# Causal attentions of a three-layer decoder: spare projections tied to heads by issue order, their weights' low parts on GpSimd, and two more output tiles begun early

## The chip, the core and the metric

One NeuronCore of one Trainium2 chip runs the whole program in one launch. The metric is device time in microseconds (us) of that core. A profile comes from one execution of its own, whose time is given beside its span.

## What is computed

One sequence of 512 tokens, width 1024, goes through three layers, each with a mixer, a cross attention to 256 memory tokens and a feed-forward part. The mixers of the first and the third layer are causal attentions, and the change is in these two. Cut to that:

```python
def _hybrid_mixer(h, ...):                 # first layer
    qa, ka, va, qb, kb, vb, fl, ga, gb = split(h @ w_in)
    # 4 differential heads: two softmaxes each, (a1 - lam * a2) @ va
    # 8 forgetting-gate heads: softmax(qb kb^T / 8 + cum_q - cum_k, causal) @ vb
    merged = sigmoid(ga) * (ya @ w_diff_out) + sigmoid(gb) * (yb @ w_fox_out)
    return merged @ w_o

def mla_attention(h, ...):                 # third layer, 16 heads
    cq, ckv, k_pe = split(h @ w_dq_dkv)    # 384, 256 and 32 columns
    q = rmsnorm(cq) @ w_uq                 # per head 64 plain and 32 rotary columns
    k_nope, v = split(rmsnorm(ckv) @ w_ukv)
    s = (q_nope k_nope^T + q_pe k_pe^T) / sqrt(96)
    return concat(softmax(s, causal) @ v) @ w_o
```

Each cross attention needs keys and values `mem_n @ w_kv` of the memory, which depend on nothing else.

## The kernel before

**Numbers.** Every matrix is split into a high part (rounded by ScalarE) and a low part (the rest), and each product is three matmuls: high by high, low by high, high by low (`mm3`, L96 to L100). `weights` (L85) loads a tile of weights in pieces of up to 512 columns by SyncE's DMA queue into `raw` (6 buffers), casts the high part `wh` on ScalarE (L92) and subtracts the low part `wl` (L93) on VectorE, or on the engine that it is given. `wh` and `wl` have 3 buffers each. `proj` runs a projection: eight 128-row tiles by three, 24 matmuls of 512 columns.

**Banks.** PSUM has eight: `mm` 3 (projections), `s` 2 (scores), `tp` 2 (transposes), `pv` 1.

**A head.** For each of four query tiles: scores into an `s` bank (L340, or L603 and L604 in the first layer); `soft_rows` takes the masked maximum on VectorE (L278), scales it on GpSimd (L280, 128x1) and takes the exponential on ScalarE (L281); `soft` divides by the sum (L711, L712); `pt_fill` transposes on TensorE (L293) and copies high and low part out (L300, L301). Then `pv64` multiplies by V (L319 to L322) and adds the two halves into `y` (L325, L326), once per head. `pt_alloc` zeroes two blocks per head on GpSimd (L286). In the third layer `mla` subtracts the low part of a head's keys on GpSimd too (L1087).

**What sets the order.** The program is written as one list, and a planner at compile time lays it out for each engine: of the instructions that are ready in its own account of time, with a buffer for what they write, the one that stands first in the list is issued. On the chip each engine then takes its instructions in that fixed order. Work that waits for nothing is thus issued early, into any gap, however late it stands in the list.

**First layer (`mixer`).** Value projections, four differential heads, then eight forgetting-gate heads in four pairs; `qk_tiles` projects queries and keys of a pair (two projections), and the next pair's stand behind the pair in the list. After the heads come the gate projections: `gates(m)` makes two (columns of `ga` and `gb`), for m = 0 to 3 before anything that needs the heads' outputs. They depend on the normed input alone. `gated` multiplies a gate's sigmoid by the output projection `w_ab` of the first or the second kind of heads.

**Third layer (`mla`).** Five latent tiles are projected in order, m = 0 to 2 for queries and 3, 4 for keys and values, with the sum of squares of each kind in `acc`; `rstd` and `bcast` turn it into a norm by two small groups of matmuls (L115, L140). The key/value norm multiplies the keys of each pair (L1081) and V; the query norm goes into the tables that multiply the queries. Then come 16 heads in eight pairs: per two pairs one `proj_tok4` for V, per pair a key projection (6 matmuls), per head a query projection (9 matmuls, L348). Behind each pair stands one job for the last layer's cross attention, `mem_k` or `mem_v` in turn: 48 matmuls of 256 columns with two tiles of 1024 weight columns, and a store from GpSimd's queue. `mem_begin` prepares the memory behind the first pair.

**Output projection (`out_proj`).** Eight output tiles; the first `lead` of them are begun with the first `first` head pairs' outputs, before the last ones are there: three in `mm` banks, two in `s` banks. With `first=6` such a lead is 18 matmuls, its low parts are on GpSimd, and 6 more matmuls end it. In `mla` the leads stand behind all heads in the list. `split_y` (L78, L79) splits the heads' outputs.

Of the kernel before, what the change touches and what calls it, by code (L numbers as in the profile page):

```python
# [48 lines left out]
class Build:  # L49
# [46 lines left out]
    def mm3(self, out, l, r, start, stop):  # L96
        mm = self.nc.tensor.matmul
        mm(out, l[0], r[0], start=start, stop=False)  # L98
        mm(out, l[0], r[1], start=False, stop=False)  # L99
        mm(out, l[1], r[0], start=False, stop=stop)  # L100
# [235 lines left out]
    def scores(self, q, k, i):  # L336
        Sp = self.p("s")
        n = max(256, P * (i + 1))
        qs = slice(P * i, P * (i + 1))
        self.mm3(Sp[:, :n], (q[0][:, qs], q[1][:, qs]), (k[0][:, :n], k[1][:, :n]), True, True)  # L340
        return Sp
# [52 lines left out]
    def out_proj(self, chunks, ys, x, norm, gains, lead=0, first=4):  # L394

        h = first
        pss = []  # L400
        for m in range(lead):
            w = self.weights(chunks[m][:, :h * P], h * P, self.nc.gpsimd)
            ps = self.p("mm" if m < 3 else "s")
            self.proj(ps, w, ys[:h], stop=False)
            pss.append(ps)
        for m in range(KT):
            if m < lead:
                w = self.weights(chunks[m][:, h * P:], (len(ys) - h) * P)
                ps = pss[m]
                self.proj(ps, w, ys[h:], start=False)  # L410
            else:
                w = self.weights(chunks[m], len(ys) * P)
                ps = self.p("mm")
                self.proj(ps, w, ys)
            self.nc.vector.tensor_add(x[m], x[m], ps)
            self.norm_tile(norm, m, x[m], gains(m))
        self.norm_end(norm)
# [135 lines left out]
    def mixer(self, norm, x, nnorm, gains):  # L553
# [5 lines left out]
        def qk_tiles(name, h, bias=None):  # L559
# [4 lines left out]
            for i in range(2):  # L564
                ps = self.p("mm")
                self.proj(ps, self.weights(a[name][2 * h + i], 1024), xs)
# [31 lines left out]
        def scores(qk, hh, i):  # L598
            Sp = self.p("s")
            n = max(256, P * (i + 1))  # L600
            qs = slice(P * i, P * (i + 1))
            q, k, q2, k2 = (t[hh] for t in qk)
            nc.tensor.matmul(Sp[:, :n], q[:, qs], k[:, :n], start=True, stop=False)  # L603
            nc.tensor.matmul(Sp[:, :n], q2[:, qs], k2[:, :n], start=False, stop=True)  # L604
            return Sp
# [32 lines left out]

        Vb = self.proj_tok(a["w_vb"], 4, xs, r, "B", stacked=True)
        for pr in range(4):  # L640
            qk = nxt
            y = self.t("E")
            for hh in range(2):
                h = 2 * pr + hh
                PT = self.pt_alloc()
                for i in range(4):
                    self.soft(scores(qk, hh, i), i, self.mask, 0.125, PT)
                self.pv64(Vb[h // 4], PT, h, y)
# [12 lines left out]
        def gates(m, tag):  # L661
            gs = []
            for i in range(2):
                w = self.weights(a["w_gate"][2 * m + i], 1024)
                ps = self.p("mm")
                self.proj(ps, w, xs)
# [22 lines left out]
        early = [gates(m, "x") for m in range(4)]  # L689
# [332 lines left out]
    def mla(self, norm, x, nnorm, gains, mstats):  # L1022
# [3 lines left out]
        lat = []  # L1026
        acc = [self.t("acc"), self.t("P")]
        for m in range(5):
# [7 lines left out]
            lat.append((H, L))  # L1036
# [6 lines left out]
        cq, ckv = lat[:3], lat[3:]  # L1043
# [25 lines left out]
        ys = []  # L1069
        kv1 = None  # L1070
        for qt in range(4):
            V = self.proj_tok4(a["ukv_v"][qt], ckv, rkv, "xl")
            for pr in range(2):
# [9 lines left out]
                for hh in range(2):  # L1083
# [6 lines left out]
                    for i in range(4):  # L1090
                        self.soft(self.scores(q, kb, i), i, self.mask, scale, PT)
                    self.pv64(V, PT, 2 * pr + hh, y)
                ys.append(y)
                if kv1 is None:
                    kv1 = self.mem_begin("mem_2", "mem1", "kv1", ["xh"] * 8, mstats)
                (self.mem_k if pr == 0 else self.mem_v)(kv1, qt)
        self.out_proj([a["mla_o"][m] for m in range(KT)], self.split_y(ys), x, nnorm, gains, lead=5, first=6)
# [208 lines left out]
```

## Time and profile before

| | us |
|---|---|
| median of 3 runs (2336.34 to 2337.86) | 2336.62 |
| the profiled execution | 2336.24 |
| its span | 2334.3 |
| mean granted TensorE clock of the span | 0.992 |

The span runs from the first to the last instruction of the profiled execution; its own time is 1.9 us more. Engines are PE (TensorE matmul), PEld (its weight loads, which overlap), DVE (VectorE), ACT (ScalarE), POOL (GpSimd) and SP (SyncE, which issues most DMAs); a small q behind the name is the engine's sequencer. L12 is line 12 of the kernel. Tiles stand as out<-in by the program's names, so `pmm` is a bank of tag `mm`. A matmul's duration contains its way through the pipeline: two that follow each other overlap, and what one costs is read from the distance of their starts. The granted clock is 1.00 at 2.4 GHz and 0.5 at 1.2 GHz. Some matmul records are missing from a trace.

### The profile page before, as it was taken

To read this page: it belongs to the slowest core of one execution; us is meant where nothing else is said; L and a number is where in the kernel's file an instruction comes from. 1 tells how busy PE (TensorE), PEld (TensorE's weight loads), DVE (VectorE), ACT (ScalarE), POOL (GpSimd) and SP (SyncE) were. 2 spreads that over 40 slices of the span, in tenths; PEclk is the share of its full clock that TensorE was granted. 3 is DMA by queue.
4 is the path that set the end of the run, shared out by engine and by line. 5 is a ranking of instruction groups with operands and counts; after the bars stand their busy time and mean duration, and the time that the engine had idled before them with its cause. 6 is when DMAs were issued, how large, how long until landed. Compare 5 with 4: busy or idle time off the path is not lost.

```text
span 2334.3 us, 32205 instructions
## 1 busy us (share of the span) xinstructions
PE 2286.1 (98%) x11454; PEld 1935.8 (83%) x11454; DVE 1407.3 (60%) x2581; ACT 1038.8 (45%) x2064; POOL 561.9 (24%) x672
## 2 busy tenths in 40 slices
PE   8999989999999999989999999999999999999998
PEld 8888868888888888878888888887997888888887
DVE  6586774556645444966656654546997656555443
ACT  6476753455323225444543332235776454332222
POOL 5323211113201105983121110011234121110002
PEclk9999999999999999989999999999999999999999
DMA  8322123313332233343123333332321313333232
GB/s 302 108 72 74 63 91 108 105 53 124 100 99 94 96 100 109 99 145 119 62 97 100 96 94 99 97 98 91 122 90 62 102 50 111 100 99 97 93 93 70
DMA packets 130528, 232.50 MB, mean 100 GB/s; under 512 B 15078, under 2 KB 25446, under 8 KB 130240
## 3 DMA queue, kind: packets, MB, share of 16 engines
q1 hardware_dynamic: 127472, 221.41, 29.6%
q0 software_dynamic: 2752, 8.81, 1.0%
q8 instruction: 90, 1.47, 0.3%
q14 instruction: 70, 0.57, 0.1%
q10 hardware_dynamic: 144, 0.23, 0.0%
HBM read 221.93 MB, written 9.71 MB: 99 GB/s over the span
## 4 chain that ended last, share of the span: by engine, by line
PE 54%; DVE 1%; ACT 1%; issue 0%; DVEq 0%; POOL 0%; ACTq 0%
PE pmm L98 16%; PE pmm L99 16%; PE pmm L100 15%; PE ps L98 1%; PE ps L99 1%; PE ps L100 1%; PE ptp L293 1%; PE ppv L320 0%; PE ptp L140 0%; PE ppv L98 0%; PE ppv L100 0%; PE ppv L99 0%; PE ptp L534 0%; PE ppv L319 0%; PE ptp L115 0%; DVE E L1180 0%
## 5 line engine op out<-in xcount | busy, mean ns | idle before, releaser
L92 ACT CAST wh<-raw 128x512 fp32r<-128x512 f32 (+1 forms) x816 | 454.2, 601 | 780.7 <-PE pmm L99 564.2
L93 DVE TENSOR_TENSOR wl<-raw,wh 128x512 fp32r<-128x512 f32 (+1 forms) x719 | 514.3, 741 | 196.0 <-ACT wh L92 194.4
L100 PE MATMUL pmm<-xh,wl 128*128 128x512 f32 (+1 forms) x1624 | 626.2, 386 | 0.0
L98 PE MATMUL pmm<-xh,wh 128*128 128x512 f32 (+1 forms) x1624 | 626.1, 386 | 0.0
L99 PE MATMUL pmm<-xl,wh 128*128 128x512 f32 x1560 | 609.5, 391 | 0.0
L98 PEld LDWEIGHTS pmm<-xh,wh 128*128 128x128 f32 x1624 | 303.9, 187 | 61.3 <-DVE x L668 0.2
L100 PEld LDWEIGHTS pmm<-xh,wl 128*128 128x128 f32 x1624 | 303.9, 187 | 61.0
L99 PEld LDWEIGHTS pmm<-xl,wh 128*128 128x128 f32 x1560 | 291.7, 187 | 60.7
L99 PE MATMUL pmm<-B,wh 128*128 128x512 f32 (+1 forms) x698 | 263.1, 378 | 0.5 <-DVE B L79 0.5
L98 PE MATMUL pmm<-A,wh 128*128 128x512 f32 (+1 forms) x578 | 217.9, 384 | 2.9 <-ACT A L78 2.9
L100 PE MATMUL pmm<-A,wl 128*128 128x512 f32 (+1 forms) x578 | 220.2, 384 | 0.0
L982 POOL TENSOR_TENSOR tmp<-tmp,rbc 128x512 f32<-128x512 f32 x44 | 57.4, 1306 | 492.2 <-ACT tmp L981 492.2
L99 PEld LDWEIGHTS pmm<-B,wh 128*128 128x128 f32 x698 | 133.2, 191 | 24.1 <-DVE B L79 0.9
L158 POOL TENSOR_TENSOR acc<-acc,tmp 128x512 f32<-128x512 f32 x55 | 79.8, 1452 | 249.6 <-ACT tmp L157 248.9
L93 POOL TENSOR_TENSOR wl<-raw,wh 128x512 fp32r<-128x512 f32 (+1 forms) x97 | 120.7, 1269 | 74.4 <-ACT wh L92 50.8
L98 PEld LDWEIGHTS pmm<-A,wh 128*128 128x128 f32 x578 | 108.2, 188 | 23.6 <-ACT A L78 3.3
L100 PEld LDWEIGHTS pmm<-A,wl 128*128 128x128 f32 x578 | 108.4, 188 | 20.4
L1004 DVE TENSOR_TENSOR x<-x,pmm 128x512 f32<-128x512 f32 x45 | 30.9, 687 | 136.3 <-PE pmm L100 136.3
L99 PE MATMUL pmm<-D,wh 128*128 128x512 f32 x288 | 112.0, 389 | 0.0
L98 PE MATMUL pmm<-E,wh 128*128 128x512 f32 x280 | 108.9, 389 | 0.0
L100 PE MATMUL pmm<-E,wl 128*128 128x512 f32 x280 | 108.9, 389 | 0.0
L281 ACT ACTIVATE P<-P,sm 128x128 f32<-128x128 f32 (+3 forms) x128 | 72.2, 564 | 52.1 <-POOL sm L280 51.0
(427 smaller groups left out, 3878.1 us busy)
## 6 DMA issues: line engine op xcount, KB each, us to landing
raw<-in_up SPq DMA_DIRECT2D x176, 256.0 KB, 2.7
raw<-in_w SPq DMA_DIRECT2D x128, 256.0 KB, 2.7
raw<-in_down SPq DMA_DIRECT2D x80, 256.0 KB, 2.7
raw<-in_kv_k SPq DMA_DIRECT2D x48, 256.0 KB, 3.0
raw<-in_kv_v SPq DMA_DIRECT2D x48, 256.0 KB, 3.0
raw<-in_w_gate SPq DMA_DIRECT2D x32, 256.0 KB, 2.9
raw<-in_xq SPq DMA_DIRECT2D x32, 256.0 KB, 2.7
raw<-in_pc_in SPq DMA_DIRECT2D x24, 256.0 KB, 2.7
```

What stands on the lines that cost most here:

```text
L92: self.nc.scalar.copy(H[:, sl], raw)
L93: (eng or self.nc.vector).tensor_sub(L[:, sl], raw, H[:, sl].bitcast(F32))
L98: mm(out, l[0], r[0], start=start, stop=False)
L99: mm(out, l[0], r[1], start=False, stop=False)
L100: mm(out, l[1], r[0], start=False, stop=stop)
L158: (nc.vector if last else nc.gpsimd).tensor_add(acc, acc, q)
L281: nc.scalar.activation(P_[:, :n], P_[:, :n], AF.Exp, bias=nb, scale=scale, accum_out=sums[:, sc:sc + 1])
L293: nc.tensor.transpose(tp[:, j, :], P_[:, j * P:(j + 1) * P], self.ident)
L982: nc.gpsimd.tensor_mul(cc, cc, norm.rb)
L1004: nc.vector.tensor_add(x[m], x[m], ps)
```

## The change

- `mm3` returns its last matmul, and the score helpers keep it (`last_s`). `tc.issue_after(ins)` binds the instructions of its block that are on `ins`'s engine to be issued behind `ins`, in issue order only, without a wait for its result. All uses here bind TensorE's instructions.
- The two gate projections of m = 0 to 3 are bound to the eight forgetting-gate heads, one each, behind the last matmul of the head's first scores. Their weights' low parts, and those of the query and key projections of these heads (`bias` is given there), are subtracted on GpSimd.
- In `mla` the key/value latents are projected first, and the two `acc` buffers change places. The jobs 0 to 3 (`mem_k`) and 4 to 7 (`mem_v`) are bound behind the first scores of heads 1, 3, 5, 7, 9, 10, 12 and 13, with both tiles' low parts on GpSimd; `mem_begin` stands behind head 0.
- `out_proj` begins seven tiles in `mla`, the sixth and seventh in the `tp` banks. The first three are bound behind scores of tile 0 and 2 of head 14 and tile 1 of head 15. The number of matmuls stays as it was.

```diff
@@ -97,7 +97,7 @@
         mm = self.nc.tensor.matmul
         mm(out, l[0], r[0], start=start, stop=False)
         mm(out, l[0], r[1], start=False, stop=False)
-        mm(out, l[1], r[0], start=False, stop=stop)
+        return mm(out, l[1], r[0], start=False, stop=stop)
     def proj(self, ps, w, xs, off=0, m=P, start=True, stop=True):
@@ -337,7 +337,7 @@
         Sp = self.p("s")
         n = max(256, P * (i + 1))
         qs = slice(P * i, P * (i + 1))
-        self.mm3(Sp[:, :n], (q[0][:, qs], q[1][:, qs]), (k[0][:, :n], k[1][:, :n]), True, True)
+        self.last_s = self.mm3(Sp[:, :n], (q[0][:, qs], q[1][:, qs]), (k[0][:, :n], k[1][:, :n]), True, True)
         return Sp
     def head_tile(self, w, xs, rb, off=0):
@@ -391,7 +391,7 @@
                 outs.append(self.stack(ps[:, v, :], r[:, 2 * u + v:2 * u + v + 1], tag))
         return outs
-    def out_proj(self, chunks, ys, x, norm, gains, lead=0, first=4):
+    def out_proj(self, chunks, ys, x, norm, gains, lead=0, first=4, pins={}):
@@ -399,10 +399,13 @@
         h = first
         pss = []
         for m in range(lead):
-            w = self.weights(chunks[m][:, :h * P], h * P, self.nc.gpsimd)
-            ps = self.p("mm" if m < 3 else "s")
-            self.proj(ps, w, ys[:h], stop=False)
-            pss.append(ps)
+            with ExitStack() as c:
+                if m in pins:
+                    c.enter_context(self.tc.issue_after(pins[m].ins))
+                w = self.weights(chunks[m][:, :h * P], h * P, self.nc.gpsimd)
+                ps = self.p("mm" if m < 3 else "s" if m < 5 else "tp")
+                self.proj(ps, w, ys[:h], stop=False)
+                pss.append(ps)
         for m in range(KT):
             if m < lead:
                 w = self.weights(chunks[m][:, h * P:], (len(ys) - h) * P)
@@ -563,7 +566,7 @@
             res, second = [], [[None, None], [None, None]]
             for i in range(2):
                 ps = self.p("mm")
-                self.proj(ps, self.weights(a[name][2 * h + i], 1024), xs)
+                self.proj(ps, self.weights(a[name][2 * h + i], 1024, nc.gpsimd if bias else None), xs)
                 t = self.t("tmp")
                 nc.vector.tensor_mul(t, ps, rb)
                 X0, X1 = self.t("A", dt=F32R), self.t("A", dt=F32R)
@@ -601,7 +604,7 @@
             qs = slice(P * i, P * (i + 1))
             q, k, q2, k2 = (t[hh] for t in qk)
             nc.tensor.matmul(Sp[:, :n], q[:, qs], k[:, :n], start=True, stop=False)
-            nc.tensor.matmul(Sp[:, :n], q2[:, qs], k2[:, :n], start=False, stop=True)
+            self.last_s = nc.tensor.matmul(Sp[:, :n], q2[:, qs], k2[:, :n], start=False, stop=True)
             return Sp
         ys = []
@@ -636,6 +639,7 @@
             ys.append(y)
             nxt = qk_tiles("w_qka", h + 1) if h < 3 else qk_tiles("w_qkb", 0, bias)
+        begun = []
         Vb = self.proj_tok(a["w_vb"], 4, xs, r, "B", stacked=True)
         for pr in range(4):
             qk = nxt
@@ -645,6 +649,8 @@
                 PT = self.pt_alloc()
                 for i in range(4):
                     self.soft(scores(qk, hh, i), i, self.mask, 0.125, PT)
+                    if i == 0:
+                        begun.append(self.last_s)
                 self.pv64(Vb[h // 4], PT, h, y)
             ys.append(y)
             if pr < 3:
@@ -658,12 +664,15 @@
             slots += [d[:, S * j:S * (j + 1)] for j in range(3)]
         slots += [self.t("T", dt=F32R) for _ in range(6)]
-        def gates(m, tag):
+        def gates(m, tag, begun=None):
             gs = []
             for i in range(2):
-                w = self.weights(a["w_gate"][2 * m + i], 1024)
+                w = self.weights(a["w_gate"][2 * m + i], 1024, nc.gpsimd if m < 4 else None)
                 ps = self.p("mm")
-                self.proj(ps, w, xs)
+                with ExitStack() as c:
+                    if begun:
+                        c.enter_context(self.tc.issue_after(begun[2 * m + i].ins))
+                    self.proj(ps, w, xs)
                 t = self.t(tag)
                 nc.vector.tensor_mul(t, ps, rb)
                 gs.append(t)
@@ -686,7 +695,10 @@
             self.split(gs[0], H, L)
             merged.append((H, L))
-        early = [gates(m, "x") for m in range(4)]
+        early = []
+        for m in range(4):
+
+            early.append(gates(m, "x", begun))
         for i in range(2):
             for m in range(4):
                 gated(early[m], m, i)
@@ -1023,9 +1035,9 @@
         nc, a = self.nc, self.a
         xs, rb, r = norm.xs, norm.rb, norm.r
         scale = 1.0 / math.sqrt(96)
-        lat = []
-        acc = [self.t("acc"), self.t("P")]
-        for m in range(5):
+        lat = {}
+        acc = [self.t("P"), self.t("acc")]
+        for m in (3, 4, 0, 1, 2):
             w = self.weights(a["dq"][m], 1024)
             ps = self.p("mm")
             self.proj(ps, w, xs)
@@ -1033,14 +1045,14 @@
             tag = "B" if m < 3 else "A"
             H, L = self.t(tag, dt=F32R), self.t(tag, dt=F32R)
             self.split_scaled(ps, g, H, L)
-            lat.append((H, L))
+            lat[m] = (H, L)
             self.square_into(acc[m // 3], ps, m in (0, 3), m in (2, 4))
             if m == 2:
                 rqb = self.bcast(self.rstd(acc[0], 384, pre=r), tag="ty")
             elif m == 4:
                 rkv = self.rstd(acc[1], 256, pre=r)
                 rkvb = self.bcast(rkv, tag="G")
-        cq, ckv = lat[:3], lat[3:]
+        cq, ckv = [lat[m] for m in range(3)], [lat[m] for m in (3, 4)]
         w = self.weights(a["dpe"], 512)
         ps = self.p("mm")
         self.proj(ps[0:64, :], w, xs, m=64)
@@ -1066,8 +1078,17 @@
             nc.scalar.copy(t[no, :], rqb[no, :])
             nc.vector.tensor_mul(t[pe, :], rqb[pe, :], self.cs[pe, :])
             csr.append(t)
-        ys = []
+        ys, tiles = [], []
         kv1 = None
+        mem = lambda j: (self.mem_k if j < 4 else self.mem_v)(kv1, j % 4, (nc.gpsimd, nc.gpsimd))
+
+        def jobs(h):
+
+            j = {1: 0, 3: 1, 5: 2, 7: 3, 9: 4, 10: 5, 12: 6, 13: 7}.get(h)
+            if j is not None:
+                with self.tc.issue_after(tiles[4 * h].ins):
+                    mem(j)
+
         for qt in range(4):
             V = self.proj_tok4(a["ukv_v"][qt], ckv, rkv, "xl")
             for pr in range(2):
@@ -1089,12 +1110,15 @@
                     PT = self.pt_alloc()
                     for i in range(4):
                         self.soft(self.scores(q, kb, i), i, self.mask, scale, PT)
+                        tiles.append(self.last_s)
                     self.pv64(V, PT, 2 * pr + hh, y)
+                    if kv1 is None:
+                        kv1 = self.mem_begin("mem_2", "mem1", "kv1", ["xh"] * 8, mstats)
+                    jobs(2 * p_ + hh)
                 ys.append(y)
-                if kv1 is None:
-                    kv1 = self.mem_begin("mem_2", "mem1", "kv1", ["xh"] * 8, mstats)
-                (self.mem_k if pr == 0 else self.mem_v)(kv1, qt)
-        self.out_proj([a["mla_o"][m] for m in range(KT)], self.split_y(ys), x, nnorm, gains, lead=5, first=6)
+        lead = [(14, 0), (14, 2), (15, 1)]
+        self.out_proj([a["mla_o"][m] for m in range(KT)], self.split_y(ys), x, nnorm, gains, lead=7, first=6,
+                      pins={m: tiles[4 * h + i] for m, (h, i) in enumerate(lead)})
         return kv1
     def run(self):
```

## Rows read from the trace of the kernel before

**Rows 1.** Busy time of TensorE over the whole span (busy us, share, instructions).

```profile
PE 2286.1 (98%) x11454; PEld 1935.8 (83%) x11454; DVE 1407.3 (60%) x2581; ACT 1038.8 (45%) x2064; POOL 561.9 (24%) x672
```

**Rows 2.** Windows: length, busy us of five engines, granted clock, DMA share, GB/s.

```profile
223.80:291.60 67.80, 67.80 (x351) 57.10 (x350) 50.65 (x141) 46.20 (x103) 15.62 (x35) 1.00 0.22 69
291.60:312.70 21.10, 14.79 (x73) 10.24 (x72) 18.31 (x59) 14.26 (x39) 4.99 (x16) 0.92 0.04 13
...
1614.00:1626.10 12.10, 9.01 (x44) 7.63 (x45) 7.51 (x15) 8.46 (x16) 2.58 (x3) 0.86 0.16 51
1626.10:1635.30 9.20, 9.20 (x62) 8.38 (x61) 6.01 (x20) 5.87 (x13) 1.34 (x4) 1.00 0.38 129
...
1768.50:1796.10 27.60, 25.39 (x137) 20.45 (x137) 21.11 (x64) 19.99 (x52) 13.87 (x22) 1.00 0.09 31
1796.10:1826.00 29.90, 24.51 (x110) 19.11 (x109) 17.21 (x41) 13.70 (x33) 4.25 (x9) 0.89 0.21 67
1693.90:1742.40 48.50, 48.50 (x322) 44.21 (x321) 44.70 (x125) 34.34 (x88) 14.21 (x32) 1.00 0.28 88
```

**Rows 3.** Windows of TensorE's instructions on `pmm` alone: length, busy us (matmuls), clock.

```profile
223.80:291.60 67.80, 53.57 (x216) 1.00 0.22 69
291.60:312.70 21.10, 0.00 (x0) 0.92 0.04 13
...
1626.10:1635.30 9.20, 7.80 (x48) 1.00 0.38 129
```

**Rows 4.** Lines of VectorE: the add closing a head, 291.6 to 312.7; 1693.9 to 1742.4.

```profile
L326 DVE TENSOR_TENSOR E<-ppv,ty 64x512 f32<-64x512 f32 x3 | 2.1, 691 | 1.5 <-ACT ty L325 1.4
...
L326 DVE TENSOR_TENSOR E<-ppv,ty 64x512 f32<-64x512 f32 x4 | 2.7, 686 | 0.1
```

**Rows 5.** Waits of TensorE, 291 to 313 us (in total, times, longest).

```profile
PE ps L603 <- DVE sm L278: 3.7, 7, 0.9
PE ppv L322 <- DVE D L301: 1.3, 1, 1.3
```

**Rows 6.** Waits of TensorE, 1602 to 1626 us.

```profile
PE pmm L98 <- DVE tmp L1081: 2.4, 1, 2.4
PE ptp L140 <- DVE st L131: 0.8, 1, 0.8
```

**Rows 7.** Waits of TensorE, 1768 to 1826 us.

```profile
PE ptp L293 <- DVE D L301: 2.9, 2, 2.6
PE pmm L98 <- ACT A L78: 2.9, 2, 2.1
```

**Rows 8.** Timeline of TensorE: start, us, instruction; two projections, then MLA's first two heads.

```profile
849.78 0.39 PE L98 MATMUL pmm<-A,wh 128*128 128x512 f32 x1
...
850.46 0.39 PE L98 MATMUL pmm<-A,wh 128*128 128x512 f32 x1
...
1624.06 0.28 PE L98 MATMUL pmm<-xh,wh 128*128 128x256 f32 x1
1624.18 0.28 PE L99 MATMUL pmm<-xh,wh 128*128 128x256 f32 x1
...
1626.09 0.28 PE L98 MATMUL ps<-T,A 128*128 128x256 f32 x1
...
1635.29 0.28 PE L98 MATMUL ps<-T,A 128*128 128x256 f32 x1
```

**Rows 9.** Lines of VectorE, 1693.9 to 1742.4 us: low parts of weights (busy us, mean ns).

```profile
L93 DVE TENSOR_TENSOR wl<-raw,wh 128x512 fp32r<-128x512 f32 x14 | 10.3, 746 | 1.1 <-ACT wh L92 1.1
...
L93 DVE TENSOR_TENSOR wl<-raw,wh 128x256 fp32r<-128x256 f32 x2 | 0.8, 414 | 0.0
```

**Rows 10.** The page's groups: low parts of weights on GpSimd, whole span.

```profile
L93 POOL TENSOR_TENSOR wl<-raw,wh 128x512 fp32r<-128x512 f32 (+1 forms) x97 | 120.7, 1269 | 74.4 <-ACT wh L92 50.8
```

**Rows 11.** Timeline of GpSimd, 1794 to 1800 us.

```profile
1794.71 4.10 POOL L93 TENSOR_TENSOR wl<-raw,wh 128x512 fp32r<-128x512 f32 x4
```

**Rows 12.** Timeline of VectorE, 1796 to 1801 us.

```profile
1798.15 0.94 DVE L93 TENSOR_TENSOR wl<-raw,wh 128x256 fp32r<-128x256 f32 x1
```

## The prediction

> **What bounds the kernel now.** The first view is the busy table: TensorE is busy for 2286.1 us of a span of 2334.3 [rows 1], so only its idle time, and the time in which it runs at half clock, can be won. The windows say where that lies in the stretches that the diff touches [rows 2]. In the eight forgetting-gate heads, TensorE has no gap from 223.8 to 291.6 us, then 14.79 busy of 21.10: 6.31 idle, at a granted clock of 0.92. In the latent attention (MLA), 1614 to 1626.1 has 3.09 idle at 0.86, 1626.1 to 1635.3 none, 1768.5 to 1796.1 has 2.21 idle, and 1796.1 to 1826 has 5.39 idle at 0.89. A clock below 1.00 is a stretch of the 1.2 GHz level among 2.4 GHz; it loses (1 − granted) × stretch: 1.69 + 1.69 + 3.29 = 6.7 us. With the idle (17.0, and 0.8 just before 1614 [rows 6]) some 24 us are at stake.
>
> Next, what was done in the full stretch. 216 projection matmuls (pmm) ran from 223.8 to 291.6 us, and none from 291.6 to 312.7 [rows 3]. 216 is nine projections of 24: all eight early gates and one query/key projection. The spare work is spent by head 3, and heads 4 to 6 run bare: three closing adds in 21.1 us, so 7.0 us a head [rows 4], of which TensorE works 14.79 / 3 = 4.9. What it then waits for is the softmax: score banks that the VectorE maximum (L278) has to free, and the copies of the transposes [rows 5]. In MLA the memory's key and value jobs are the spare work, spent before the last four heads.
>
> **The change, part by part.**
>
> *Gates behind heads.* A 512-column matmul costs 0.68 / 3 = 0.227 us [rows 8], a gate of 24 of them 5.4. One per head makes 4.9 + 5.4 = 10.3 us of TensorE against a chain of 7.0: TensorE becomes the bound in all eight heads, and the clock has no cause to fall. Gates moved away from heads 0 to 3 only let those heads run sooner, since the total of matmuls is the same. At stake 6.31 + 1.69 = 8.0. I leave 1.3, one wait as long as the longest of this stretch [rows 5], for head 0, where only one gate covers the first softmax: **−6.7 us**.
>
> *Latents in the order 3, 4, 0, 1, 2.* Before, the key/value latent came last, and the query projections waited 2.4 us for L1081, which needs its norm, after 0.8 for that norm's own broadcast [rows 6]. Now that norm is ready three projections (16 us) earlier. The query norm is late instead, behind the rotary key, V and key projections, which hide it as they hid the other. −3.2 and −1.69 of clock: **−4.9 us**.
>
> *Memory jobs behind heads 1, 3, 5, 7, 9, 10, 12, 13.* The first job ran around head 0: 17 matmuls up to its first scores at 1626.09 and 31 more up to head 1's at 1635.29. At 0.12 us each [rows 8] its 48 matmuls are 5.7 us, and they filled head 0's softmax in a stretch without a gap [rows 2, 3]. Now head 0 has no cover but the next pair's key projection (6 × 0.227 = 1.4). The next pair's query weights must queue for one of three weight buffers behind the job's own two, so they are late too. Bounds: 0 if that projection still comes, and 5.7 + 1.7 for a clock drop if nothing does. Nearest is the job without the key projection: **+4.3 us**. The other jobs stand where a pair's projections leave room; heads 12 and 13, bare before (2.21 idle), get two: **−1.7 us**, with 0.5 left.
>
> *Three leads pinned into heads 14 and 15, two more in the transposes' banks.* A lead is 18 matmuls, 4.1 us. Three pinned ones give 12.3 us of cover where 2.6 us were spent on a transpose whose bank VectorE had not freed, and the two in the transposes' banks give 8.2 after the last transposes, over the 2.1 us wait for the last head's split [rows 7]. They start no earlier than that bank is free, which is before the last PV product, so they can cover it. At stake 5.39 + 3.29 = 8.7; with 1.3 left: **−7.4 us**. The two outputs' weights come in three pieces instead of two (one more ScalarE cast each), beside a full TensorE: 0.
>
> *Low parts on GpSimd.* 8 query/key, 8 gate and 8 × 2 job weights make 64 subtractions of 128x512, and two new leads 4 smaller ones. Each leaves VectorE (0.746 us [rows 9], 47.7 in all) and takes 1.27 on GpSimd [rows 10], 81 us over stretches where it is mostly idle. Behind them on its queue stand the 128x1 scaling of every softmax (L280), MLA's key low part, the zero blocks of the next head and the stores of the jobs; ScalarE's exponential waits for the scaling. Four such subtractions ran in a row for 4.10 us at 1794.71 [rows 11], just ahead of the 2.6 us wait. Bounds: 0 (where spare matmuls are at hand, as for 67.80 us in the gate stretch, a late softmax costs nothing; a gain is not excluded, as VectorE is relieved) and 2.6 per four for the 8 jobs, 20.8. Between them the nearest stretch is 1768.5 to 1796.1, where leads' low parts already share GpSimd with the heads: 2.21 idle over about ten of them, 0.22 each. Half of the jobs' and leads' 36 I take as covered: 18 × 0.22 = **+4.0 us**. The 32 others lie beside a full TensorE: 0.
>
> Sum: −6.7 − 4.9 + 4.3 − 1.7 − 7.4 + 4.0 = −12.4. The profiled execution took 2336.24 us (span 2334.3), 0.4 below the median of 2336.62; 2336.24 − 12.4 gives **2324 us**.
>
> **Where the skill speaks against it.** The row first: a 128x256 low part on VectorE took 0.94 us beside GpSimd's four [rows 12], against 0.41 at other times [rows 9]. The Trainium skill ("SBUF — State Buffer", Who interferes with whom) says that such a VectorE instruction and GpSimd share one port pair, an exclusive lock that blocks the loser for the whole instruction; by that rule the sum would be that of the third rival, and this row agrees with it.
>
> **The rivals.**
> 1. *The hole moves.* MLA heads without a spare job (0, 2, 4, 6, 8, 11) each idle as the bare gate heads did, 6.31 / 3 = 2.1 us: 12.6 in place of 4.3, giving 2332. For it: the same softmax, two score banks. Against: MLA heads are heavier on TensorE, 48.5 us for four with their jobs [rows 2, 4], and the pair's projections fall into the even heads. Chance 0.10.
> 2. *GpSimd becomes the wait*, slower. Each job's four subtractions hold up the scaling as at 1794.71 and cost 2.6, each gate's two half of it: 8 × 2.6 + 8 × 1.3 = 31.2 in place of 4.0, giving 2351. It outweighs the gains from (12.4 + 4.0) / 12 = 1.4 us per four. Against: that row had next to no spare matmuls beside it, the new stretches have. Chance 0.11.
> 3. *The lock.* Every one of 36 MLA subtractions delays a VectorE instruction by 0.94 − 0.41 = 0.53: 19 us, which takes back most of the 23.9 that VectorE gains there (32 × 0.746). Where a job or lead stands beside, TensorE hides it; six heads without one pay 19 / 16 each, some 7 us: 2331. Chance 0.05.
> 4. *The bindings bind nothing*, because the spare work ran that late anyway: 2336. The 216 and 0 of [rows 3] say otherwise: 0.02.
>
> **How the numbers follow.** The forecast has the rest, 0.72. A measurement of this kernel tells a change from none at about 0.2%, 4.7 us: faster is below 2331.9. The forecast's own range is 2312.4 (all 23.8 won) to 2331.9. Rivals 1, 3 and 4 end near or within 0.2%, rival 2 above. So faster 0.72, same 0.17, slower 0.11. The range 2313 to 2337 holds the forecast and rivals 1, 3 and 4, and leaves out rival 2 and the rim of the forecast.
>
> **What would show it.** Right: gate projections spread over all eight heads, one each, and idle below 2 us at clock 1.00 from head 0 to head 7; no wait for L1081 after the latents; idle between MLA's first scores and the second head's of 3 to 6 us; below 2 us from head 12 to the last split. Wrong: waits of TensorE on transposes or scores whose chain goes back to L280 behind L93 on GpSimd, a granted clock below 0.9 at MLA's first head, or gaps in the even heads that add up to the old ones.

## The result, and the profile after

The changed kernel takes 2374.91 us (median of 4 runs, 2373.77 to 2375.79) against 2337.24 of the kernel before on the same chip: a ratio of 1.0155, 95% interval 1.0143 to 1.0167. It is 37.7 us slower where the forecast was 12 faster. The profiled execution has a span of 2372.0 us; that of before had 2334.3.

The page of the changed kernel: the busy table, then two groups (columns as in [rows 1, 10]).

```profile
PE 2299.6 (97%) x11454; PEld 1941.5 (82%) x11454; DVE 1395.7 (59%) x2515; ACT 1042.2 (44%) x2066; POOL 646.0 (27%) x740
...
L93 POOL TENSOR_TENSOR wl<-raw,wh 128x512 fp32r<-128x512 f32 (+1 forms) x165 | 211.7, 1306 | 111.3 <-ACT wh L92 83.7
...
L281 ACT ACTIVATE P<-P,sm 128x128 f32<-128x128 f32 (+3 forms) x128 | 72.0, 563 | 82.4 <-POOL sm L280 81.4
```

GpSimd took over 68 low parts (165 instead of 97) and grew by 84 us, as reckoned (81). TensorE runs the same 11454 matmuls, yet is busy 13.5 us longer; by the two cuts below, some 8 us of that are half clock. In the last row, ScalarE's exponential waited 81.4 us for the scaling L280; before, the same row of the page ends in 51.0.

Where the time went, by windows of the changed kernel (columns as in [rows 2]):

```profile
226.70:297.80 71.10, 60.72 (x294) 48.51 (x293) 43.40 (x123) 45.09 (x100) 33.83 (x52) 0.95 0.20 60
...
1637.00:1645.00 8.00, 7.78 (x42) 6.38 (x42) 4.04 (x20) 3.81 (x13) 1.32 (x5) 0.70 0.01 2
1645.00:1800.00 155.00, 139.16 (x887) 123.14 (x885) 115.72 (x312) 99.72 (x243) 75.19 (x117) 0.97 0.28 85
...
227.00:350.00 123.00, 108.78 (x527) 86.87 (x526) 82.39 (x215) 75.48 (x166) 42.04 (x70) 0.97 0.19 58
1616.00:1882.00 266.00, 238.40 (x1383) 205.22 (x1382) 193.32 (x470) 165.84 (x388) 120.08 (x169) 0.96 0.28 85
```

The last two rows are cut by the work, from the first forgetting-gate scores to 10 us behind the last closing add, and from 20 us ahead of MLA's first scores to 20 behind its last closing add. The same cuts of the kernel before:

```profile
224.00:339.00 115.00, 108.11 (x538) 87.77 (x537) 88.04 (x230) 75.84 (x168) 24.94 (x54) 0.99 0.19 60
1606.00:1841.00 235.00, 224.19 (x1367) 197.20 (x1367) 194.24 (x502) 159.91 (x380) 74.18 (x132) 0.98 0.30 96
```

The gate heads became 8 us longer, with 14.2 us idle instead of 6.9, and MLA 31 us longer, with 27.6 idle instead of 10.8 and a granted clock of 0.96 instead of 0.98 (10.6 against 4.7 us lost). The other 8 of the 31 us are busy time of TensorE that no view here takes apart. The stretch that had no gap in the gate heads (67.8 us, [rows 2]) now has 10.4 us of idle in 71.1. Over most of MLA before had no gap of note:

```profile
1640.00:1768.50 128.50, 128.49 (x875) 118.51 (x874) 115.47 (x323) 92.99 (x234) 42.21 (x87) 1.00 0.32 103
```

From 1645 to 1800 the changed kernel has 15.8 us idle, some 11 of them in heads 2, 4, 6 and 8, which have no job of their own. Two of the signs that the prediction named for its failure are plain: a granted clock below 0.9 at MLA's first head (0.70 from 1637 to 1645), and gaps in the even heads. Of the third, waits whose chain goes back to L280 behind L93, the waits are there; what they go back to is traced below.

TensorE's waits in the changed kernel, 226 to 262, 1610 to 1645 and 1645 to 1800 us (in total, times, longest):

```profile
PE ps L606 <- DVE sm L278: 5.4, 2, 3.5
...
PE ps L98 <- ACT A L78: 5.6, 1, 5.6
...
PE ps L98 <- DVE sm L278: 9.3, 10, 2.1
...
PE ps L100 <- DVE A L79: 1.7, 2, 1.5
```

The first and third are scores that wait for a bank, on which a softmax's maximum (L278) is late; the second is MLA's first scores, which wait for the split of the query; the last is scores that wait for a query's low part (L79).

### The profile page after: what moved, and what is told of

Its sections match the earlier page's. It is cut to its first block, busy times and chain, and to the rows that moved or that the text cites. A ratio compares the mean times of both kernels' runs of the same rounds, so it can differ in the third digit from the quotient of the medians.

```text
span 2372.0 us, 32212 instructions
## 1 busy us (share of the span) xinstructions
PE 2299.6 (97%) x11454; PEld 1941.5 (82%) x11454; DVE 1395.7 (59%) x2515; ACT 1042.2 (44%) x2066; POOL 646.0 (27%) x740
## 4 chain that ended last, share of the span: by engine, by line
PE 52%; DVE 2%; ACT 1%; issue 1%; POOL 0%; DVEq 0%; POOLq 0%
PE pmm L98 15%; PE pmm L99 15%; PE pmm L100 15%; PE ps L98 1%; PE ps L100 1%; PE ps L99 1%; PE ptp L293 1%; PE ptp L140 0%; PE ppv L98 0%; PE ppv L99 0%; PE ppv L100 0%; ACT wh L92 0%; PE ptp L537 0%; PE ppv L320 0%; PE ptp L115 0%
## 5 line engine op out<-in xcount | busy, mean ns | idle before, releaser
L93 DVE TENSOR_TENSOR wl<-raw,wh 128x512 fp32r<-128x512 f32 (+2 forms) x653 | 468.0, 742 | 193.1 <-ACT wh L92 190.4
L99 PE MATMUL pmm<-B,wh 128*128 128x512 f32 (+1 forms) x682 | 256.2, 376 | 0.0
L93 POOL TENSOR_TENSOR wl<-raw,wh 128x512 fp32r<-128x512 f32 (+1 forms) x165 | 211.7, 1306 | 111.3 <-ACT wh L92 83.7
L100 PE MATMUL pmm<-A,wl 128*128 128x512 f32 (+1 forms) x562 | 214.2, 384 | 0.4 <-DVE wl L93 0.4
L98 PE MATMUL pmm<-A,wh 128*128 128x512 f32 (+1 forms) x562 | 212.3, 383 | 0.0
L100 PEld LDWEIGHTS pmm<-A,wl 128*128 128x128 f32 x562 | 105.4, 188 | 20.8 <-DVE wl L93 0.8
L281 ACT ACTIVATE P<-P,sm 128x128 f32<-128x128 f32 (+3 forms) x128 | 72.0, 563 | 82.4 <-POOL sm L280 81.4
```

The source lines that it names most:

```text
L93: (eng or self.nc.vector).tensor_sub(L[:, sl], raw, H[:, sl].bitcast(F32))
L100: return mm(out, l[1], r[0], start=False, stop=stop)
L281: nc.scalar.activation(P_[:, :n], P_[:, :n], AF.Exp, bias=nb, scale=scale, accum_out=sums[:, sc:sc + 1])
```

## The experiments

Each kernel is set against the kernel before on its own chip, whose median was 2337.2 to 2339.7; the difference of the two medians stands as +18.4 us or the like, and costs of parts are differences of these. First, two theories: GpSimd's queue does it, or the bindings.

### All low parts back on VectorE, bindings kept

```diff
-self.proj(ps, self.weights(a[name][2 * h + i], 1024, nc.gpsimd if bias else None), xs)
+self.proj(ps, self.weights(a[name][2 * h + i], 1024), xs)
-w = self.weights(a["w_gate"][2 * m + i], 1024, nc.gpsimd if m < 4 else None)
+w = self.weights(a["w_gate"][2 * m + i], 1024)
-mem = lambda j: (self.mem_k if j < 4 else self.mem_v)(kv1, j % 4, (nc.gpsimd, nc.gpsimd))
+mem = lambda j: (self.mem_k if j < 4 else self.mem_v)(kv1, j % 4)
```

> The changed kernel with all 64 low parts back on VectorE; every binding, the latents' order and the seven leads stay. If the binding costs the time (theory B: the spare work stands in one block behind a head's first scores and is missing in the heads without it), the 38 us stay almost whole: 2360 to 2380 us, with the holes of the even MLA heads (2.5 to 3 us of TensorE each) still there. If GpSimd's queue costs it (theory G: the scaling of the maximum waits behind the subtractions), most comes back: 2325 to 2342 us.

2356.53 us, +18.4; ratio 1.0082 [1.0066, 1.0099]. Half of the loss is left.

### No binding, low parts on GpSimd; and neither

The first takes away all three uses of `issue_after`; the second takes away the bindings and the low parts on GpSimd, so that the order of the latents, the places of the jobs in the list and the seven leads are left.

```diff
-early.append(gates(m, "x", begun))
+early.append(gates(m, "x"))
-with self.tc.issue_after(tiles[4 * h].ins):
-    mem(j)
+mem(j)
-lead=7, first=6, pins={m: tiles[4 * h + i] for m, (h, i) in enumerate(lead)})
+lead=7, first=6)
```

> The changed kernel without any binding; low parts stay on GpSimd, the order of the latents, the jobs' places in the list and seven leads stay. Theory B: 2325 to 2342 us, no hole over 1 us before MLA's last heads. Theory G: 2360 to 2380 us, with the scaling L280 still waiting up to 4 us behind L93 on GpSimd.

2337.66 us, −0.4; 1.0002 [0.9992, 1.0011].

> The changed kernel without bindings and with the 64 low parts on VectorE; the latents' order, seven leads and the jobs' places in the list stay. If GpSimd costs time only where bound work leaves a softmax bare, this equals the run without bindings within 5 us: 2331 to 2338 us. If GpSimd's subtractions cost the 18 us by themselves that they cost beside the bindings: some 2320 us.

2330.27 us, −7.4; 0.9967 [0.9953, 0.9980].

The four corners: +37.7 (both), +18.4 (bindings), −0.4 (GpSimd), −7.4 (neither). The bindings cost 26 us by themselves; GpSimd's low parts cost 7 without them and 19 beside them, so 12 us come only where both are there. Both theories hold, that of the bindings more. The cuts by the work, of the kernel with the bindings only, then with neither:

```profile
224.00:340.00 116.00, 107.42 (x537) 87.25 (x536) 87.84 (x230) 76.40 (x168) 23.87 (x54) 0.99 0.19 58
1606.00:1863.00 257.00, 236.66 (x1385) 202.95 (x1383) 198.86 (x503) 165.86 (x389) 79.82 (x137) 0.97 0.28 88
```

```profile
226.00:342.00 116.00, 109.60 (x536) 88.78 (x535) 87.71 (x230) 76.08 (x168) 24.33 (x54) 0.96 0.19 59
1612.00:1840.00 228.00, 222.57 (x1376) 196.44 (x1375) 193.15 (x498) 161.30 (x383) 80.89 (x137) 1.00 0.31 97
```

The bindings add 29 us to MLA and nothing to the gate heads. GpSimd's 19 beside them (spans of 2372.0 and 2353.1) are 3 ahead of the first gate scores, 7 in the gate heads and 9 in MLA; what lies between and behind the cuts is the same within 0.1 us. The exponential's row of the page, of the kernel with the bindings only, with GpSimd only, and with neither, does not add up in this way:

```profile
L281 ACT ACTIVATE P<-P,sm 128x128 f32<-128x128 f32 (+3 forms) x128 | 72.0, 563 | 78.9 <-POOL sm L280 77.9
```

```profile
L281 ACT ACTIVATE P<-P,sm 128x128 f32<-128x128 f32 (+3 forms) x128 | 72.1, 563 | 65.3 <-POOL sm L280 64.3
```

```profile
L281 ACT ACTIVATE P<-P,sm 128x128 f32<-128x128 f32 (+3 forms) x128 | 72.2, 564 | 54.4 <-POOL sm L280 53.8
```

GpSimd's low parts raise the wait for the scaling L280 by 10.5 us without the bindings, but only by 3.5 beside them, where they cost most. In the changed kernel's two cuts it is 18.0 and 44.3 us, against 19.3 and 43.4 with the bindings only. So the wait for the scaling does not by itself account for the 19 us.

GpSimd's fixed order does hold the scaling up, as its timeline at the first gate head shows (start us, us):

```profile
226.23 5.02 POOL L93 TENSOR_TENSOR wl<-raw,wh 128x512 fp32r<-128x512 f32 x4
231.22 0.22 POOL L280 TENSOR_SCALAR sm<-sm 128x1 f32<-128x1 f32 x1
```

The maximum that L280 scales was there at 227.28 us; a scaling of 0.22 us stood 3.9 us behind four low parts. Little of this reaches TensorE here. Lines of ScalarE, VectorE and TensorE up to TensorE's next hole:

```profile
229.89 1.14 ACT L92 CAST wh<-raw 128x512 fp32r<-128x512 f32 x2 [3.56 <-issue]
231.47 0.40 ACT L281 ACTIVATE P<-P,sm 128x128 f32<-128x128 f32 x1 [0.45 <-POOL sm L280]
...
237.29 0.69 DVE L677 TENSOR_TENSOR x<-pmm,rbc 128x512 f32<-128x512 f32 x1 [4.50 <-PE ptp L293]
...
239.18 1.64 DVE L577 TENSOR_TENSOR A<-tmp,A 64x512 fp32r<-64x512 f32 x1
...
241.13 0.54 DVE L278 CUSTOM_DVE_ANT_0 P<-ps,mask 128x384 f32<-128x384 f32 x1
...
241.73 0.38 PE L606 MATMUL ps<-A,A 128*128 128x256 f32 x1 [3.55 <-DVE sm L278]
```

The first line is two casts of weights, which stood ahead of the exponential on ScalarE until 231.03; so the exponential waited only 0.45 us for the scaling. The scores at 241.73 wait for the maximum at 241.13. In VectorE's order that stands behind a gate's multiplication (L677), which waited 4.50 us for TensorE, and behind L577, which took 1.64 us beside GpSimd's low parts where the kernel with the bindings only has 0.69. That second way, VectorE's longer instructions, is measured under "The lock" below.

### Latents alone, leads alone, both

Each is the kernel before with that part of the change, the leads without `pins`.

```diff
-for m in range(5):
+for m in (3, 4, 0, 1, 2):
...
```

> The kernel before with the latents in the order 3, 4, 0, 1, 2 alone. By the prediction's step the 3.2 us of idle and 1.7 us of clock before MLA's first query projections go: 2332 us. If the query norm, now last, takes the place of the key/value norm as the wait (in the changed kernel TensorE waited 5.6 us for a split A L78 there): 2337 to 2341 us.

2333.55 us, −4.6; 0.9980 [0.9971, 0.9990]. Of the waits of [rows 6] one is left, in this kernel from 1595 to 1632 us:

```profile
PE pmm L98 <- DVE tmp L1081: 1.3, 1, 1.3
```

Its window from 1614 to 1626.1 us has a granted clock of 1.00 instead of 0.86.

```diff
-ps = self.p("mm" if m < 3 else "s")
+ps = self.p("mm" if m < 3 else "s" if m < 5 else "tp")
...
-... lead=5, first=6)
+... lead=7, first=6)
```

> The kernel before with seven leads in MLA's output projection instead of five, nothing bound. By the prediction's step the last 2.1 us wait for the split of the last head goes: 2334 to 2335 us. If the two more leads only take weight buffers and GpSimd's time from the last heads: 2337 to 2341 us.

2335.63 us, −2.5; 0.9988 [0.9979, 0.9998]. Its window at the end of MLA:

```profile
1796.10:1826.00 29.90, 27.46 (x126) 21.81 (x125) 13.34 (x34) 13.50 (x33) 9.56 (x15) 0.89 0.20 62
```

Idle 2.4 instead of 5.4 [rows 2], at the same clock of 0.89.

> The kernel before with the latents' order and seven leads alone. If the two gains add (0.2% and 0.12% alone): 2330 to 2332 us. If both fill the same wait at the end of MLA: 2333 to 2336 us.

2329.44 us, −8.2; 0.9964 [0.9951, 0.9976]: the two add up. At the end of MLA its half clock is gone too:

```profile
1792.00:1822.00 30.00, 28.70 (x139) 23.05 (x138) 14.12 (x37) 14.13 (x35) 9.52 (x12) 1.00 0.23 70
```

### Jobs behind other heads

The jobs' and the query/key low parts are on VectorE (the gates' stay on GpSimd), the jobs stand behind the even heads, which had none.

```diff
-j = {1: 0, 3: 1, 5: 2, 7: 3, 9: 4, 10: 5, 12: 6, 13: 7}.get(h)
+j = {0: 0, 2: 1, 4: 2, 6: 3, 8: 4, 10: 5, 12: 6, 13: 7}.get(h)
...
```

> The changed kernel with the low parts of queries, keys and jobs on VectorE (those of the gates stay on GpSimd) and the first six memory jobs bound behind heads 0, 2, 4, 6, 8, 10 instead of 1, 3, 5, 7, 9, 10. Theory: the even head is bare, because the projections of its pair have to come before it and the job comes after it; with the job behind its own first scores MLA's holes of 20.6 us fall to 8 or less and the time to 2338 to 2346 us. Rival: a block of 48 matmuls leaves holes behind whichever head it is bound to: 2350 us or more.

2359.54 us, +21.9; 1.0093 [1.0079, 1.0107]: no better than behind the odd heads (+18.4); MLA's cut is 259 us against 257. The theory that the choice of head is at fault falls; a job bound as one block costs about the same behind either.

### Pieces instead of blocks

A block of 24 or 48 matmuls covers the softmax of one score tile; the other three of the head have none. Here, with all low parts on VectorE and the leads free, each gate is bound in four pieces of six matmuls, one behind each score tile of its head, and each job in eight pieces behind the eight tiles of its pair.

```diff
-if i == 0:
-    begun.append(self.last_s)
+begun.append(self.last_s)
...
-with ExitStack() as c:
-    if begun: c.enter_context(self.tc.issue_after(begun[2 * m + i].ins))
-    self.proj(ps, w, xs)
+for k in range(8):
+    with ExitStack() as c:
+        if begun: c.enter_context(self.tc.issue_after(begun[4 * (2 * m + i) + k // 2].ins))
+        sl = slice(k * P, (k + 1) * P)
+        self.mm3(ps, (w[0][:, sl], w[1][:, sl]), xs[k], k == 0, k == 7)
...
```

> Low parts on VectorE, leads not bound, but gates and jobs bound in pieces: a gate's 24 matmuls six behind each of the four score tiles of its head, a job's 48 six behind each of the eight score tiles of a pair, and the job placed in the list behind the pair. Theory (the block is what costs): the holes of the gate heads fall below 4 us and those of MLA below 8, 2322 to 2332 us. Rival (held-back work occupies the three weight buffers, and the next pair's query weights come late): MLA's holes stay at 15 us or more, 2345 to 2360 us.

2338.56 us, +0.9; 1.0003 [0.9994, 1.0012]. Its two cuts by the work:

```profile
226.00:336.00 110.00, 106.16 (x536) 87.18 (x536) 86.87 (x230) 75.55 (x168) 23.48 (x54) 0.98 0.20 62
1602.00:1846.00 244.00, 227.71 (x1376) 199.42 (x1375) 197.74 (x503) 163.80 (x388) 79.26 (x136) 0.99 0.29 92
```

The gate heads are 5 us shorter than before, with 3.8 idle in place of 6.9; MLA is still 9 us longer, with 16.3 idle in place of 10.8.

The gate pieces alone, jobs and leads free:

> No binding in MLA, low parts on VectorE, latents in the new order, seven leads, and the gates bound in pieces of six matmuls behind each score tile of their heads. By the run in pieces the first layer's heads end 4 to 5 us sooner than unbound: 2325 to 2328 us. If what they win is paid back behind them: 2329 to 2332 us.

**2325.04 us, −14.7; 0.9935 [0.9923, 0.9948]**, the fastest kernel of this study. Its cuts:

```profile
226.00:336.00 110.00, 106.14 (x537) 87.15 (x536) 86.84 (x230) 75.98 (x168) 23.06 (x54) 0.98 0.20 62
1606.00:1834.00 228.00, 222.59 (x1376) 196.45 (x1375) 193.19 (x498) 161.30 (x383) 80.89 (x137) 1.00 0.31 97
```

MLA with free jobs: 5.4 us idle, clock 1.00. The binding of the jobs, in pieces, costs the 16 us between the last two kernels, which is also the difference of their MLA cuts (244 and 228).

The leads' binding without the others (low parts on VectorE):

> The run without bindings and with low parts on VectorE, plus the changed kernel's binding of the first three leads behind heads 14 and 15. If the leads belong to the bound work that costs time: 2334 us or more. If the last two heads have room for them, as the prediction had it: 2326 to 2331 us.

2329.77 us, −9.9; 0.9959 [0.9945, 0.9973]. Against −7.4 without it that is no loss, and with intervals that overlap no sure gain. Its cuts, the base for what bound gates and jobs cost:

```profile
224.00:340.00 116.00, 109.91 (x536) 89.04 (x536) 87.83 (x230) 76.31 (x168) 24.19 (x54) 0.96 0.19 58
1610.00:1839.00 229.00, 222.83 (x1375) 197.31 (x1373) 194.07 (x497) 161.16 (x383) 81.54 (x137) 0.99 0.31 96
```

### Why bound jobs cost in MLA

First suspect: the weights of a bound job hold two of the three weight buffers while the next pair's query weights wait. Here a job's weights go through the two buffers of tag `T` that MLA's keys leave free (four of six hold keys), one piece of 512 columns at a time; first with the jobs in pieces, then as one block behind the heads of the change:

```diff
+def piece(self, src, i):
+    H, L = self.t("T", dt=F32R), self.t("T", dt=F32R)
+    raw = self.t("raw")
+    self.nc.sync.dma_start(raw, src[:, S * i:S * i + S])
+    self.split(raw, H, L)
+    return H, L
...
```

> The run in pieces (low parts on VectorE, gates and jobs in pieces, leads not bound), with the jobs' weights in two idle buffers of tag T, 512 columns at a time, so that held-back jobs no longer occupy the three weight buffers that the next pair's queries need. If those buffers are what still costs in MLA (16.3 us of holes, mostly TensorE waiting for the split of a late query projection): holes of 8 us or less, 2322 to 2330 us. If it is something else: 12 us or more, 2335 to 2340 us.

2348.05 us, +8.4; 1.0038 [1.0024, 1.0051].

> Jobs again in one block behind the first scores of heads 1, 3, 5, 7, 9, 10, 12, 13, but with weights of their own in the T buffers; gates in pieces, low parts on VectorE, leads not bound. If the late query weights alone made the holes, MLA's fall to 8 us or less, about 2325 to 2332 us. If the block makes most of them: 14 us or more, 2338 to 2352 us.

2374.33 us, +34.6; 1.0149 [1.0133, 1.0164]. Both are slower than with the shared buffers (+0.9 in pieces, +18.4 as blocks with the gates and leads bound too), so the theory gets no support. It is not excluded: with two buffers, which also take the jobs' split results, a job's pieces come one behind the other, so the test brought a wait of its own.

Next: only the first job is freed, or only the last two are bound.

```diff
-mem = lambda j: (self.mem_k if j < 4 else self.mem_v)(kv1, j % 4, after=tiles[8 * j:8 * j + 8])
+mem = lambda j: (self.mem_k if j < 4 else self.mem_v)(kv1, j % 4, after=tiles[8 * j:8 * j + 8] if j else None)
```

> The kernel `spread` (2338.6 us) with the first memory job set free again; jobs 1 to 7 stay bound in pieces over the pairs 1 to 7. Theory S (the start): most of what the bound jobs cost in MLA is that the first job no longer lies between the latents and the second head. In `spread` TensorE is idle for 5.9 us before the first scores against 1.3 in `gate_pieces`, and loses 1.4 + 1.7 and 1.4 + 1.7 us (idle + half clock) around heads 0 and 1 against 0: 4.6 + 6.2 = 10.8 us. With job 0 free those go: 2327 to 2331 us, idle before the first scores under 2 us. Rival E (every bound job): each bound job holds back the next pair's projections in TensorE's fixed order, so the seven others cost about 1.5 us each whatever the first does: 2334 to 2338 us, with the holes of pairs 1 to 7 as they were (6.6 us of idle from head 2 to head 15) or larger.

2338.1 us, −0.7; 0.9998 [0.9989, 1.0008]. The start is not the cause by itself: the gap ahead of the first scores is gone, but the spare work now ends before head 0. Windows of `pmm` alone over 20 us from the first scores on, of the kernel with the gate pieces alone and of this one:

```profile
1626.00:1646.00 20.00, 15.56 (x94) 1.00 0.43 134
```

```profile
1623.00:1643.00 20.00, 5.65 (x28) 0.91 0.24 75
```

With all jobs free, the second job and a V projection stand there, a pair ahead of where a binding puts them. Two places of this kernel's PE timeline show what is missed:

```profile
1633.21 0.39 PE L98 MATMUL ps<-T,A 128*128 128x256 f32 x1 [3.30 <-DVE sm L278]
...
1734.67 0.51 PE L98 MATMUL ps<-T,A 128*128 128x256 f32 x2 [1.63 <-ACT A L78]
...
1736.91 0.41 PE L98 MATMUL pmm<-wh,xh 128*128 128x256 f32 x1
```

The first is a bare softmax in head 0. The second recurs at the start of pairs: the pair's first scores wait for the split of its query, and the job that could fill the gap comes at 1736.91, because it is bound behind just those scores. Such waits from 1650 to 1840 us:

```profile
PE ps L98 <- ACT A L78: 3.5, 3, 1.6
PE ps L100 <- DVE A L79: 1.9, 2, 1.5
```

The kernel with free jobs has none of either in that stretch.

For the other, `if j else None` becomes `if j > 5 else None`:

> The kernel `gate_pieces` (2325.0 us) with the last two memory jobs bound in pieces, behind the score tiles of pairs 6 and 7; jobs 0 to 5 and the leads stay free. In `gate_pieces` TensorE is idle for 1.5 + 0.2 + 0.3 + 1.3 = 3.3 us around heads 11 to 14 and 0.5 at head 8. Theory C (cover): bound there, where no later pair's projections are left to be held back, spare jobs fill these gaps: 2321 to 2324 us. Rival E (every bound job costs, by about 1.5 us): 2326 to 2330 us. No change (2324.5 to 2325.5) would mean that the last gaps are waits that no spare matmul reaches.

2327.93 us, −10.8; 0.9954 [0.9938, 0.9971]: 4 behind the kernel with free jobs, with intervals that overlap, and no gain. One stretch of it, and the same of the kernel with free jobs:

```profile
1700.00:1760.00 60.00, 55.08 (x334) 46.97 (x334) 49.73 (x150) 41.02 (x106) 18.36 (x44) 0.97 0.21 68
```

```profile
1700.00:1760.00 60.00, 59.54 (x411) 54.75 (x410) 52.04 (x148) 44.80 (x114) 23.03 (x44) 1.00 0.30 95
```

The two jobs that now lie under the last heads had filled this stretch; 4.5 us more of gaps appear there. Spare matmuls are a fixed sum, and the planner's own spread was at least as good.

## Why the prediction was wrong

The sum was −12.4; measured are +37.7. Step by step:

- **Gates behind heads, −6.7.** The reading of the rows was right: spare matmuls were spent early and heads 4 to 6 ran bare. The step that failed is "TensorE becomes the bound in all eight heads". It compared sums per head (10.3 against 7.0), but a gate as one block covers one of the four tiles of a head. With the low parts on VectorE the gate heads take the same 116 us with bound blocks as without any binding; in pieces they take 110, and the kernel gains 7 us (−7.4 to −14.7).
- **Latents, −4.9.** Right by itself: −4.6, from the places named [rows 6], clock included. Beside bound jobs it was not: the 5.6 us wait of MLA's first scores follows the query norm's broadcast, TensorE's last work ahead of it. The norm that the V and key projections were to hide was hidden by the free first job too. The kernels with the new order and the first job bound wait 4.5 to 5.8 us for the query there, those with that job free do not. No run has bound jobs with the old order.
- **Jobs behind heads, +4.3 and −1.7.** The mis-sized step, and the largest. From bound leads alone (−9.9) to bound leads, gates and jobs (+18.4) it is 28 us, and MLA's cut grows by just that, from 229 to 257 us; the gate heads take 116 in both. Of the 28 us, 14 are idle time and 5 half clock. The hole between the first scores and head 1's was forecast, at 4.3; in the changed kernel it lies ahead of the first scores (5.6 us), and from there to head 1's, at 1640.66, TensorE has no gap of note but runs at a granted clock of 0.50. "The other jobs stand where a pair's projections leave room" failed: those pairs had no gap before, and a bound block lies behind scores, while the boundary of the pairs and the other tiles run bare. The rival "the hole moves" had the right places, and its 12.6 is near the 14 of idle time; half clock and longer busy time doubled it.
- **Leads, −7.4.** −2.5 on their own, −3.6 beside the new order of the latents. The idle fell from 5.4 to 2.4, but the half-clock stretch stayed, which I had counted as won; in the version with both parts it went as well. Binding three of them costs nothing and gains nothing sure.
- **GpSimd's low parts, +4.0.** +7 without the bindings and +19 beside them, both within the bounds (0 to 20.8) but not at the value taken. I had costed 32 of them, in the gate stretch, at nothing because TensorE was full there; the bindings opened gaps in it, and it lost 7 us. The rival "GpSimd becomes the wait" had the sign (2351). Its mechanism, the scaling in GpSimd's queue, is seen without the bindings (in MLA's cut ScalarE's wait for it goes from 24.0 to 30.6 us); beside them it hardly grew, so that most of the 19 us came in another way.
- **The lock** was priced nearly right and given too small a chance. Over MLA's cut, VectorE's instructions of the same shapes took 13.8 us longer in all in the changed kernel than with the bindings only (for each shape, its count times the difference of the means). That is 0.43 for each of the 32 low parts that went to GpSimd there; the rival had 0.53. Without the bindings it is 14.3 us. VectorE is still busy for 5.5 us less in that cut (193.3 against 198.9), as it has lost those low parts; but the longer instructions stand in the chain of the softmax and of the queries. From 1645 to 1800 us, softmax divisions (L724), splits of the queries (L79) and low parts, first in the changed kernel, then with the bindings only:

```profile
L724 DVE TENSOR_SCALAR P<-P,sm 128x512 f32<-128x512 f32 x12 | 11.8, 984 | 0.2
L79 DVE TENSOR_TENSOR A<-tmp,A 128x512 fp32r<-128x512 f32 x11 | 11.2, 1022 | 2.1 <-ACT A L78 2.1
L93 DVE TENSOR_TENSOR wl<-raw,wh 128x512 fp32r<-128x512 f32 x11 | 8.3, 763 | 1.6 <-issue 0.8 <-ACT wh L92 0.6
```

```profile
L93 DVE TENSOR_TENSOR wl<-raw,wh 128x512 fp32r<-128x512 f32 x37 | 24.6, 686 | 3.1 <-ACT wh L92 3.0
L79 DVE TENSOR_TENSOR A<-tmp,A 128x512 fp32r<-128x512 f32 x12 | 9.2, 771 | 0.2 <-ACT A L78 0.2
...
L724 DVE TENSOR_SCALAR P<-P,sm 128x512 f32<-128x512 f32 x12 | 8.1, 672 | 0.1
```

Two places show how this reaches TensorE. In the first, a division that takes 0.49 us at 1814.20 took 2.45 beside two low parts on GpSimd; a query's split (L79) stood behind it on VectorE, and TensorE waited 2.15 us for that, up to 1803.34. Its waits for such splits are 3.8 us in MLA's cut, against 0.2 with the bindings only. In the second, ahead of MLA's first scores, the two multiplications by the query norm took 3.35 us beside two low parts on GpSimd, against 1.4 in the other kernel; the wait there is 5.6 us against 4.5. That the longer instructions make most of GpSimd's 9 us in MLA is argued from these places, not shown by a run of its own.

```profile
1799.05 2.50 POOL L93 TENSOR_TENSOR wl<-raw,wh 128x512 fp32r<-128x512 f32 x2
...
1799.39 2.45 DVE L724 TENSOR_SCALAR P<-P,sm 128x512 f32<-128x512 f32 x1
...
1631.12 3.35 DVE L1079 TENSOR_TENSOR B<-ty,G 64x512 f32<-64x512 f32 x2 [1.34 <-ACT ty L148]
```

No rival alone holds the result. The bindings' holes, GpSimd's queue and the lock were given 0.10, 0.11 and 0.05, and never their sum.

What stays open: how GpSimd's 19 us divide between its queue and VectorE's longer instructions, which no run separates; and whether bound jobs would cost less with the old order of the latents, or with enough buffers of their own.

## What to carry to other kernels

Cover is counted per gap, not per head: bound spare matmuls helped here only in pieces that stood beside each wait, and a binding behind scores can't fill the gap ahead of them. Moving spare work takes it from where it lay, so show first that its old place can do without it; here that was so for the gates (the projections piled up in heads 0 to 3) and not for the jobs (no gap in six pairs). Work that moves to an idle engine is priced by what it does to the others, by what stands behind it in that engine's order and by how much longer its neighbours' instructions take beside it, rather than by the engine's busy share.

## What was not expected of the hardware

An engine that was busy for 27% of the span (GpSimd) cost 7 to 19 us, though it had time to spare. Its 0.22 us scaling once stood 3.9 us behind weights' low parts, but the larger sign is on VectorE, whose instructions took 13.8 us longer in MLA's cut. And a short idle time costs twice where the clock falls: behind the 5.6 us wait at 1635.77 us in the changed kernel, 8 us ran at a granted clock of 0.70, some 2.4 us more. The shared port is seen in single rows, as [rows 12] and the division at 1799.39 us, which ended 0.29 us behind GpSimd's second low part; in the mean it came to 0.08 to 0.31 us an instruction. The Trainium skill ("SBUF — State Buffer", Who interferes with whom) calls it an exclusive lock for the whole instruction, and the row at 1799.39 agrees: 2.45 us, about as long as the two low parts beside it.
